# A decoder block on one core: the planner that orders VectorE and ScalarE gets other transfer times and deadlines that are spread out

## The chip, the core and the metric

The kernel runs on one core of a Trainium2 chip. A core has five engines, each with an instruction stream of its own that runs strictly in order: TensorE (PE in the profile; its weight loads are listed as PEld), VectorE (DVE), ScalarE (ACT), GpSimd (POOL) and SyncE (SP). SP and POOL issue nearly all of this kernel's DMAs; the issues themselves are rows SPq, POOL and ACTq. The engines wait for each other, and for DMAs, with semaphores: an instruction whose input is not there holds back everything behind it on its own engine.

The metric is the device time of one execution in microseconds, the median of several runs. The output must agree with the reference.

## The reference, cut to what matters

One decoder block (DEPTH is 1) on 512 tokens with a width of 2048, all in float32:

```python
D_MODEL = 2048; SEQ = 512; MLA_HEADS = 8; GDN_HEADS = 8; D_FF = 5632

c_act = silu(c)
mod = c_act @ w_ada + b_ada                      # six vectors of 2048
sh_a, sc_a, gt_a, sh_f, sc_f, gt_f = split(mod, 6)
h = rmsnorm(x, norm_mix) * (1 + sc_a) + sh_a
p = h @ w_in                                     # queries, keys, values, gates of both mixers
y_a = mla(...) @ w_o_mla                         # latent attention, causal softmax
y_b = gated_delta_net(...) @ w_o_gdn             # chunked gated delta rule
g_a, g_b = split(sigmoid(gate_logits), 2)
x = x + gt_a * ((g_a * y_a + g_b * y_b) @ w_o)
h = rmsnorm(x, norm_ffn) * (1 + sc_f) + sh_f
gate, up = split(h @ w_gate_up, 2)               # w_gate_up: 2048 x 11264
x = x + gt_f * ((silu(gate) * up) @ w_down)      # w_down: 5632 x 2048
return rmsnorm(x, final_norm)
```

## The kernel before

**Precision and tiling.** Activations lie transposed in SBUF, 128 features on the partitions and the 512 tokens along the row. Every float32 operand of a large product is cut in two rounded halves: ScalarE casts a tile to float32r (`hi`, `xh`), VectorE subtracts that from the tile and keeps the rest (`lo`, `xl`). TensorE then does three products for each pair, hi with hi, hi with lo, lo with hi (`three`, line 566). So before a weight tile can be used it goes through a chain: a load on SP's queue into a buffer `raw` or `raws` (five of them, `RAWS`), a cast on ScalarE into one of four `hi` buffers, and a subtraction on VectorE into one of four `lo` buffers (`SPLITS`).

**Strassen products.** The products with w_o, w_gate_up and most of w_down are done in Strassen form, seven products in place of eight (`strassen`, line 2284, for w_o and w_down; `big`, line 2087, for w_gate_up). In `strassen` a unit of work, of which there are eight for each set of 512 output columns, loads one weight tile `raws` of 128x1024 (four blocks of 256 columns). VectorE adds up combinations of the blocks into a tile `sums`; then both are cut in halves: a `hi` and a `lo` of 128x768 from `raws`, a `hi` and a `lo` of 128x1024 from `sums`. The matmuls of this stage write the banks `m`: rows `m<-xh,hi`, `m<-xh,lo` and `m<-xl,hi`. The activation side of w_down's product is made by `sums_down`: it loads blocks `a11`, `a21`, `a22`, `a12` from a scratch tensor in DRAM, `f_dram` (`fetch_a`; rows `a<-f_dram`), adds them up into combinations, and cuts each of these in `xh` (ScalarE) and `xl` (VectorE). The same four tile names hold both the loaded block and a combination of it. The part of w_down that isn't in Strassen form (banks `dn`) ends with four ScalarE instructions `y<-dn,gt_ffn`, which empty its four banks, and four accumulating DMAs into `x2_dram`.

**Stages in time.** First the modulation and the statistics of x (`head`; a product with w_ada is a custom VectorE instruction, `rawm<-rawm,cbc`, of which there are 192; they are spread over the kernel as side work wherever VectorE has room), then w_in with both mixers, among it attention, 32 items of one head and 128 queries each (`attention`, line 1450). An item's probabilities are transposed on TensorE (bank `pT`), copied to SBUF by VectorE or ScalarE in turn (`pT<-pT`), and multiplied with the values (`yT<-pT,V`). Then w_o in Strassen form, whose last set adds into the tiles `x2` (`x<-g`, `x<-p`; the plain remainder of it is `x<-wo`) and squares them (`squares`, tile `sq`) for the norm; a matmul with ones (`hss`) adds up the squares, and VectorE makes the reciprocal root (`rs`). Then w_gate_up, w_down, and the last norm with the output in rows.

**What sets the order.** No engine call is issued where the code makes it. `Writer` (line 287) records each as an `Op` in `Score`; `Op.durations` (line 165) gives it two numbers, `pace`, how long it keeps its engine, and `seen`, when its result can be used. At the end `Score.issue` (line 449) does three things:

- `depend` (line 294) finds from the accesses which operation needs which. Two accesses of one DRAM tensor meet when their ranges overlap.
- `latest` (line 333) gives each operation a deadline. TensorE's operations are due when TensorE would get to them if it ran without a pause; everything else is due early enough for its users, with a DMA's lead put at 2200 ns + bytes/300.
- `order` (line 362) runs through a model of the engines. TensorE, GpSimd and SyncE keep the order in which the code recorded them. For VectorE and ScalarE (`CHOSEN`, line 276) it takes, of the operations that are ready within `LOOK` of the engine's next free moment, the one with the earliest deadline. In this model one bus carries all DMAs at 355 bytes per ns, and a DMA's issue costs 60 ns on SyncE and 600 ns on GpSimd.

The result is a fixed order for each engine, in which the operations are issued (line 454). So nearly all instructions have line 454 in the profile, and groups are told apart by tile. Since the real order is fixed, what the model got wrong turns up on the chip as an instruction that waits at the head of its engine while others behind it could run.

## Time and profile before

| what | us |
|---|---|
| median of the runs | 2729.58 (three runs, 2728.38 to 2730.99) |
| the profiled execution's own time | 2729.74 |
| its span, first to last instruction | 2728.0 |
| TensorE busy | 2703.5, 99% of the span |
| TensorE weight loads busy | 2352.9, 86% |
| VectorE busy | 2128.4, 78% |
| ScalarE busy | 1209.8, 44% |
| GpSimd busy | 254.5, 9% |
| mean granted TensorE clock | 0.997 |

The profiled execution took 1.74 us more than its span, which is what lies before the first and behind the last instruction. The page shows an engine's busy time over the span; the chain of work that ended last is followed back from the last instruction. The view of waits sums, for an engine, the time in which it stood still and what released it. The timeline lists instructions with their start and length in us and, in brackets, the idle time in front of them and its releaser; neighbours of one kind are drawn together as "x3". A table of windows gives busy time, the number of instructions and the granted clock of stretches of time. Names in the trace have no buffer numbers; a tile made in place of a pool named `raws` or `a11` is written `raws` or `a`.

### The profile page before, as it was taken

The page shows a single profiled execution, that of the slowest core. Times are in us where ns is not written, and L with a number is a line of the kernel's source. Part 1 is how long each engine was busy: PE and PEld are TensorE (multiplying, and loading weights), DVE is VectorE, ACT ScalarE, POOL GpSimd, SP SyncE. Part 2 cuts the span into 40 slices and gives each one's busy share as a digit, 9 for nine tenths or more (in the row PEclk, how much of TensorE's full clock was granted, in tenths as well). Part 3 has the DMA queues.
Part 4 walks back from the last instruction along what each step waited for, and adds up shares of the span by engine and source line. Part 5 has one row for each costly group of instructions (what it writes and reads, how often), then busy time and mean ns, then how long its engine had stood idle before and what let it go on. Part 6 is the DMA issues. An engine that isn't in the chain of part 4 may idle for free.

```text
span 2728.0 us, 41132 instructions
## 1 busy us (share of the span) xinstructions
PE 2703.5 (99%) x15304; PEld 2352.9 (86%) x15304; DVE 2128.4 (78%) x3361; ACT 1209.8 (44%) x1717; POOL 254.5 (9%) x361
## 2 busy tenths in 40 slices
PE   9999999999999999999999999999999999999997
PEld 7888788888888888889999888888888888998997
DVE  8885666776978887688797877788878886877976
ACT  4343432442345343245573444444444455445444
POOL 0000011102101000000000000000000103013013
PEclk9999999999999999999999999999999999999999
DMA  9995555645667998524855556666565668569565
GB/s 354 349 371 181 164 179 153 213 141 165 193 177 218 319 320 298 185 88 122 279 178 160 185 198 201 207 206 207 198 212 187 217 212 186 130 195 200 144 186 166
DMA packets 315490, 562.21 MB, mean 206 GB/s; under 512 B 40772, under 2 KB 120916, under 8 KB 315288
## 3 DMA queue, kind: packets, MB, share of 16 engines
q1 hardware_dynamic: 264776, 458.99, 51.7%
q0 software_dynamic: 31872, 74.76, 10.7%
q10 hardware_dynamic: 18640, 25.83, 2.7%
q8 instruction: 120, 1.97, 0.3%
q14 instruction: 82, 0.67, 0.1%
HBM read 476.62 MB, written 83.89 MB: 205 GB/s over the span
## 4 chain that ended last, share of the span: by engine, by line
PE 95%; DMA 2%; DVE 1%; issue 1%; ACT 0%; POOL 0%; SPq 0%; POOLq 0%; ACTq 0%; DVEq 0%
PE m L454 42%; PE gb L454 6%; PE v L454 4%; PE gu L454 3%; PE z L454 3%; PE ya L454 3%; PE ga L454 3%; PE k L454 3%; PE s L454 3%; PE q L454 3%; PE yb L454 3%; PE dn L454 3%; PE qk L454 2%; PE cq L454 2%; PE ckv L454 2%; PE wo L454 1%
## 5 line engine op out<-in xcount | busy, mean ns | idle before, releaser
L454 ACT CAST hi<-raw 128x1024 fp32r<-128x1024 f32 (+2 forms) x251 | 260.3, 1038 | 482.2 <-DMA raw<-in_w_in_dram 92.5
L454 ACT CAST hi<-raws 128x1024 fp32r<-128x1024 f32 (+2 forms) x328 | 292.0, 890 | 398.3 <-PE m L454 289.2
L454 DVE TENSOR_TENSOR lo<-raws,hi 128x1024 fp32r<-128x1024 f32 (+2 forms) x328 | 332.1, 1021 | 127.6 <-ACT hi L454 124.2
L454 DVE TENSOR_TENSOR lo<-raw,hi 128x1024 fp32r<-128x1024 f32 (+2 forms) x251 | 304.5, 1215 | 126.0 <-ACT hi L454 121.5
L454 PE MATMUL m<-xh,lo 128*128 128x256 f32 x1088 | 309.7, 285 | 2.4 <-DVE lo L454 2.4
L454 PE MATMUL m<-xh,hi 128*128 128x256 f32 x1088 | 309.3, 284 | 1.9 <-ACT hi L454 1.9
L454 PE MATMUL m<-xl,hi 128*128 128x256 f32 x1088 | 308.9, 284 | 0.0
L454 DVE CUSTOM_DVE_ANT_0 rawm<-rawm,cbc 128x1024 f32<-128x1024 f32 x192 | 233.1, 1225 | 89.3 <-DMA rawm<-in_w_mod_dram 84.2
L454 ACT CAST hi<-sums 128x1024 fp32r<-128x1024 f32 x168 | 176.4, 1050 | 229.2 <-PE m L454 197.7
L454 DVE TENSOR_TENSOR lo<-sums,hi 128x1024 fp32r<-128x1024 f32 x168 | 205.5, 1223 | 74.0 <-ACT hi L454 72.7
L454 PEld LDWEIGHTS m<-xh,lo 128*128 128x128 f32 x1088 | 209.9, 193 | 3.7 <-DVE lo L454 3.5
L454 PEld LDWEIGHTS m<-xh,hi 128*128 128x128 f32 x1088 | 209.9, 193 | 2.5 <-ACT hi L454 2.4
L454 PEld LDWEIGHTS m<-xl,hi 128*128 128x128 f32 x1088 | 209.9, 193 | 0.1
L454 PE MATMUL m<-hi,h2h 128*128 128x512 f32 x480 | 189.9, 396 | 0.0
L454 PE MATMUL m<-hi,h2l 128*128 128x512 f32 x480 | 187.2, 390 | 0.0
L454 PE MATMUL m<-lo,h2h 128*128 128x512 f32 x480 | 187.1, 390 | 0.0
L454 PEld LDWEIGHTS m<-hi,h2l 128*128 128x128 f32 x480 | 90.1, 188 | 18.8
L454 PEld LDWEIGHTS m<-lo,h2h 128*128 128x128 f32 x480 | 90.3, 188 | 17.8
L454 PEld LDWEIGHTS m<-hi,h2h 128*128 128x128 f32 x480 | 90.2, 188 | 17.6
L454 PE MATMUL gb<-hh,hi 128*128 128x512 f32 x256 | 102.1, 399 | 0.0
L454 PE MATMUL gb<-hl,hi 128*128 128x512 f32 x256 | 100.0, 391 | 0.0
L454 PE MATMUL gb<-hh,lo 128*128 128x512 f32 x256 | 99.8, 390 | 0.0
(543 smaller groups left out, 7018.1 us busy)
## 6 DMA issues: line engine op xcount, KB each, us to landing
raws<-in_w_gate_up_dram SPq DMA_DIRECT2D x400, 256.0 KB, 3.6
rawm<-in_w_mod_dram SPq DMA_DIRECT2D x192, 512.0 KB, 5.4
raw<-in_w_in_dram SPq DMA_DIRECT2D x143, 512.0 KB, 4.7
raws<-in_w_down_dram SPq DMA_DIRECT2D x128, 256.0 KB, 3.7
s_dram<-raws POOLq DMA_DIRECT2D x80, 256.0 KB, 2.6
raws<-s_dram SPq DMA_DIRECT2D x80, 256.0 KB, 2.8
rawa<-in_w_in_dram SPq DMA_DIRECT2D x32, 512.0 KB, 4.5
raws<-in_w_o_dram SPq DMA_DIRECT2D x48, 256.0 KB, 2.9
```

What stands on the lines that cost most here:

```text
L454: self.tc.keep_in_program_order(op.call(*op.args, **op.kwargs))
```

## The change

All of it is in the recorder and the planner; no engine call of the kernel body is added, removed or given other operands.

- **Times of DMAs in the model.** A DMA's issue costs 540 ns on GpSimd (720 when it accumulates), 370 on ScalarE and 410 on SyncE, in place of 600 and 60. A new method `transfer` gives the time on the bus, `move`: bytes/360, times 1.85, 1.5 or 1.17 where the shortest contiguous row of the access is at most 256, 512 or 1024 bytes, and times 2.35 or 3.1 when the DMA accumulates. In `order` a DMA gets to the bus 1200 ns (GpSimd) or 1800 ns after its start, and counts as done 640 ns + `SPARE` (1000) behind its end on the bus.
- **DRAM accesses.** `Access` notes the shortest contiguous row, and for a DRAM tensor keeps the exact stretches in place of one range from the first to the last element.
- **Deadlines.** A DMA's lead is `LANDING` (3000) + `move`. `latest` runs three rounds (`ROUNDS`). After each, the deadlines on VectorE, and those on ScalarE, are gone through from the last back: none may be later than the deadline behind it less the operation's own pace. The next round takes these as caps, and so passes them on to what feeds the operation.
- **LOOK** goes from 400 to 800 ns.

```diff
     def durations(self):
         if self.dma:
-            return (600.0 if self.engine == "gpsimd" else 60.0), 0.0
+            pool = 720.0 if self.kwargs.get("accum_op") is not None else 540.0
+            return {"gpsimd": pool, "scalar": 370.0}.get(self.engine, 410.0), 0.0
...
+    def transfer(self):
+
+        row = min(a.row for a in self.reads + self.writes)
+        if self.kwargs.get("accum_op") is not None:
+            return self.bytes / 360.0 * (3.1 if row > 2048 else 2.35)
+        return self.bytes / 360.0 * (1.85 if row <= 256 else 1.5 if row <= 512 else 1.17 if row <= 1024 else 1.0)
...
-            self.parts, self.runs = (0, 1), ((off, off + sum((c - 1) * abs(s) for s, c in steps) + 1),)
+            self.parts, self.runs = (0, 1), () if self.input else self.stretches(off, steps)
...
     CHOSEN = ("vector", "scalar")
-    LOOK = 400.0
+    LOOK = 800.0
+    LANDING = 3000.0
+    ROUNDS = 3
+    SPARE = 1000.0
...
-        end, out, after = t + 5000.0, [0.0] * n, {}
-        for k in range(n - 1, -1, -1):
-            op = ops[k]
-            seen = 2200.0 + op.bytes / 300.0 if op.dma else op.seen
-            v = min([out[j] - seen for j in self.users[k] + late[k]], default=end)
-            if op.pe:
-                v = start[k]
-            elif op.engine not in self.CHOSEN:
-                v = after[op.engine] = min(v, after.get(op.engine, end) - op.pace)
-            out[k] = v
+        end, cap = t + 5000.0, [t + 5000.0] * n
+        for _ in range(self.ROUNDS):
+            out, after = [0.0] * n, {}
+            for k in range(n - 1, -1, -1):
+                op = ops[k]
+                seen = self.LANDING + op.move if op.dma else op.seen
+                v = min([out[j] - seen for j in self.users[k] + late[k]], default=end - seen)
+                if op.pe:
+                    v = start[k]
+                elif op.engine not in self.CHOSEN:
+                    v = after[op.engine] = min(v, after.get(op.engine, end) - op.pace)
+                out[k] = min(v, cap[k])
+            for e in self.CHOSEN:
+                at = end
+                for k in sorted((k for k in range(n) if ops[k].engine == e), key=lambda k: (-out[k], -k)):
+                    cap[k] = at = min(out[k], at - ops[k].pace)
         return out
...
             if op.dma:
-                bus = max(start + op.pace + 1500.0, bus) + op.bytes / 355.0
-                done[k] = bus + 500.0
+                bus = max(start + (1200.0 if op.engine == "gpsimd" else 1800.0), bus) + op.move
+                done[k] = bus + 640.0 + self.SPARE
```

**What moves.** Both kernels hold the same instructions. The orders of TensorE, GpSimd and SyncE are the same in both. On VectorE 2010 of 3361 instructions stand at another place, on average by two places and at most by 138; on ScalarE 548 of 1801, at most by 18. Three places, with the buffer numbers left in the names:

Place A is ScalarE where the plain part of w_down (`dn36_3`) ends and the Strassen product with w_down begins. `hi_3660` is the cast of the first unit's weights and `hi_3662` that of their sums; `hi_3673` and `hi_3675` belong to the second unit. The `xh` copies cut activation blocks that come from `f_dram` or are made from such blocks. Before:

```order
L454 COPY xh_3683_3823<-a21_3623_3763 128x512
L454 COPY xh_3693_3833<-a11_3618_3758 128x512
L454 COPY hi_3660_3800<-raws_3609_3749 128x768
L454 COPY xh_3698_3838<-a12_3654_3794 128x512
L454 ACTIVATE y_3655_3795<-dn36_3_3637_3777,gt_ffn_120 128x512
L454 ACTIVATE y_3656_3796<-dn36_3_3638_3778,gt_ffn_120 128x512
L454 ACTIVATE y_3657_3797<-dn36_3_3639_3779,gt_ffn_120 128x512
L454 COPY hi_3662_3802<-sums_3659_3799 128x1024
L454 COPY xh_3710_3850<-a11_3682_3822 128x512
L454 ACTIVATE y_3658_3798<-dn36_3_3640_3780,gt_ffn_120 128x512
L454 COPY hi_3673_3813<-raws_3630_3770 128x768
L454 COPY xh_3718_3858<-a12_3700_3840 128x512
```

After:

```order
L477 COPY hi_3660_3800<-raws_3609_3749 128x768
L477 COPY xh_3693_3833<-a11_3618_3758 128x512
L477 COPY xh_3683_3823<-a21_3623_3763 128x512
L477 ACTIVATE y_3655_3795<-dn36_3_3637_3777,gt_ffn_120 128x512
L477 ACTIVATE y_3656_3796<-dn36_3_3638_3778,gt_ffn_120 128x512
L477 ACTIVATE y_3657_3797<-dn36_3_3639_3779,gt_ffn_120 128x512
L477 COPY hi_3662_3802<-sums_3659_3799 128x1024
L477 COPY xh_3698_3838<-a12_3654_3794 128x512
L477 ACTIVATE y_3658_3798<-dn36_3_3640_3780,gt_ffn_120 128x512
L477 COPY hi_3673_3813<-raws_3630_3770 128x768
L477 COPY xh_3710_3850<-a11_3682_3822 128x512
L477 COPY hi_3675_3815<-sums_3672_3812 128x1024
```

`hi_3660` now stands ahead of `xh_3693` and `xh_3683` (which precede it before), and `y_3658` and `hi_3673` stand ahead of `xh_3710`, which preceded both. The next Strassen set of w_down shows the same exchange: `xh_4092` and `xh_4096`, which stood ahead of `y_4047`, `hi_4062` and `hi_4064`, now follow these, and `xh_4100` now follows `hi_4079`, ahead of which it stood. Call that place B.

Place C is VectorE at the end of w_o, ahead of the reciprocal root `rs_2098`, which needs the sum of squares `hss_2097` and so both last additions into `sq_2034`. `g1` and `p1` are Strassen results, `wo3` the banks of the remainder. Before:

```order
L454 TENSOR_TENSOR p1_2019_2159<-euvw_1971,m5_1972_2112 128x512
L454 TENSOR_TENSOR lo_2085_2225<-raw_2062_2202,hi_2084_2224 128x1024
L454 TENSOR_SCALAR x2_2010_2150<-g1_2017_2157,gt_mix_119,x2_2010_2150 128x256 x2
L454 TENSOR_SCALAR x2_2012_2152<-p1_2019_2159,gt_mneg_122,x2_2012_2152 128x256 x2
L454 TENSOR_TENSOR lo_2092_2232<-raw_2069_2209,hi_2091_2231 128x1024
L454 TENSOR_SCALAR x2_2023_2163<-wo3_2027_2167,gt_mix_119,x2_2023_2163 128x256 x2
L454 TENSOR_SCALAR x2_2025_2165<-wo3_2028_2168,gt_mix_119,x2_2025_2165 128x256 x2
L454 TENSOR_TENSOR sq_2034_2174<-sq_2034_2174,sq_2087_2227 128x512
L454 TENSOR_TENSOR sq_2034_2174<-sq_2034_2174,sq_2088_2228 128x512
L454 TENSOR_TENSOR lo_2095_2235<-raw_2076_2216,hi_2094_2234 128x1024
L454 TENSOR_TENSOR lo_2103_2243<-raw_2081_2221,hi_2102_2242 128x1024
L454 TENSOR_SCALAR rs_2098_2238<-hss_2097_2237 128x2
```

After:

```order
L477 TENSOR_TENSOR g1_2017_2157<-euvw_1971,m4_1971_2111 128x512
L477 TENSOR_TENSOR lo_2092_2232<-raw_2069_2209,hi_2091_2231 128x1024
L477 TENSOR_SCALAR x2_2023_2163<-wo3_2027_2167,gt_mix_119,x2_2023_2163 128x256 x2
L477 TENSOR_SCALAR x2_2025_2165<-wo3_2028_2168,gt_mix_119,x2_2025_2165 128x256 x2
L477 TENSOR_TENSOR sq_2034_2174<-sq_2034_2174,sq_2087_2227 128x512
L477 TENSOR_TENSOR sq_2034_2174<-sq_2034_2174,sq_2088_2228 128x512
L477 TENSOR_TENSOR lo_2095_2235<-raw_2076_2216,hi_2094_2234 128x1024
L477 TENSOR_TENSOR lo_2103_2243<-raw_2081_2221,hi_2102_2242 128x1024
L477 TENSOR_SCALAR rs_2098_2238<-hss_2097_2237 128x2
```

`p1_2019` and the two pairs of `x2_2010` and `x2_2012` are gone from this stretch; in the new order they stand behind the whole chain of `rs` and the two `diag_2101` that follow it.

Place D is VectorE in attention; the lines `ISA rawm` are the custom instruction on w_ada, and `pT_1439` is an item's copy of its transposed probabilities. Before:

```order
L454 TENSOR_REDUCE sm_114<-sc_1435_1574 128x1
L454 TENSOR_SCALAR sm_114<-sm_114 128x1
L454 TENSOR_TENSOR lo_1445_1584<-raw_1431_1570,hi_1444_1583 128x1024
L454 ISA rawm_1428_1567,parts_82<-rawm_1428_1567,cbc_128 128x1024
L454 ISA parts_82 128x1
L454 COPY pT_1439_1578<-pT_1438_1577 128x128
L454 TENSOR_TENSOR yl_1437_1576<-yT_1417_1556,yh_1436_1575 128x512
L454 TENSOR_TENSOR sc_1441_1580<-sc_1441_1580,kc_79 128x128
```

After:

```order
L477 TENSOR_SCALAR sm_114<-sm_114 128x1
L477 ISA rawm_1416_1555,parts_82<-rawm_1416_1555,cbc_128 128x1024
L477 ISA parts_82 128x1
L477 ISA rawm_1427_1566,parts_82<-rawm_1427_1566,cbc_128 128x1024
L477 ISA parts_82 128x1
L477 ISA rawm_1428_1567,parts_82<-rawm_1428_1567,cbc_128 128x1024
L477 ISA parts_82 128x1
L477 TENSOR_TENSOR yl_1437_1576<-yT_1417_1556,yh_1436_1575 128x512
L477 COPY pT_1439_1578<-pT_1438_1577 128x128
L477 TENSOR_TENSOR sc_1441_1580<-sc_1441_1580,kc_79 128x128
```

Three custom instructions on w_ada and the `yl` subtraction now stand between the item's `sm_114` and its `pT_1439`; before it was one `lo` and one custom instruction.

At the start of the kernel VectorE now takes a small cast, `strict_r`, ahead of its first custom instruction, and `hl_22`, the second half of the first activation tile, ahead of the wide part of `lo_20`, where it stood behind. At the very end, four of the row products `xo<-x2t,row` now stand between the last two steps of the final norm's `rs`, the three products with `hbc` that followed that chain stand ahead of it, and the last product with `hbc`, `x2_4344`, which stood ahead of two products and one scaling of `xo`, now stands ahead of its last two scalings.

More of the change, by code (lines that the diff above doesn't have):

```diff
@@ L163, in __init__ @@
         self.bytes = 4 * self.writes[0].total
+        self.move = self.transfer() if self.dma else 0.0
     def durations(self):
@@ L213, in __init__ @@
         self.total = self.count * steps[0][1]
+        self.row = 4
+        for s, c in reversed(steps):
+            if c > 1 and 4 * s != self.row:
+                break
+            self.row *= c
         space = str(getattr(t, "space", "")).upper()
```

## The prediction

> **What bounds the kernel now.** I read the page first, then TensorE's waits, then windows around them, then the timeline of each engine there.
>
> ```profile
> PE 2703.5 (99%) x15304; PEld 2352.9 (86%) x15304; DVE 2128.4 (78%) x3361; ACT 1209.8 (44%) x1717; POOL 254.5 (9%) x361
> PE 95%; DMA 2%; DVE 1%; issue 1%; ACT 0%; POOL 0%; SPq 0%; POOLq 0%; ACTq 0%; DVEq 0%
> ...
> PE cb L454 <- DMA crow<-in_c_dram: 3.0, 1, 3.0
> PE m L454 <- DVE lo L454: 2.4, 5, 0.8
> PE m L454 <- ACT hi L454: 1.9, 2, 1.4
> PE hss L454 <- DVE sq L454: 1.2, 2, 0.8
> ```
>
> TensorE is the chain that sets the end, with 95% of it. Its matmuls, their number and their order stay as they are. So the change can win only what TensorE loses in waits and what comes of them, plus something in the tail, and it loses wherever the new order makes TensorE wait. The waits are few. The first 3.0 us (the load of c) is no matter of order. The next three rows, 2.4 + 1.9 + 1.2, are 5.5 us, nearly all of it in three places. But a wait's idle time is not all that it costs:
>
> ```profile
> 2298.00:2309.00 11.00, 8.15 (x41) 0.69 0.46 82
> 2309.00:2320.00 11.00, 11.00 (x95) 1.00 0.42 133
> ...
> 2509.00:2524.00 15.00, 13.62 (x109) 1.00 0.54 124
> 2530.00:2545.00 15.00, 15.00 (x128) 1.00 0.41 118
> ```
>
> These are windows of TensorE's instructions into the banks `m`: length, busy time with the count, granted clock, DMA share, GB/s. In place A (ScalarE's exchange at the start of the Strassen product with w_down) 41 matmuls run in 11 us, where 95 do in the next window. The missing 54 at 11.00/95 = 0.116 us are 6.3 us. In place B, 128 - 109 = 19 are missing, at 15.00/128 = 0.117 us 2.2 us. B kept its clock; A did not.
>
> **The change, part by part.** *Place A.* TensorE, ScalarE, VectorE and SyncE, from the timeline:
>
> ```profile
> 2299.72 0.39 PE L454 MATMUL m<-xh,hi 128*128 128x256 f32 x1 [1.40 <-ACT hi L454]
> 2300.72 0.39 PE L454 MATMUL m<-xh,lo 128*128 128x256 f32 x1 [0.49 <-DVE lo L454]
> ...
> 2302.55 0.41 PE L454 MATMUL m<-xh,lo 128*128 128x256 f32 x1
> ...
> 2304.10 0.58 PE L454 MATMUL m<-xh,hi 128*128 128x256 f32 x1 [0.50 <-ACT hi L454]
> ...
> 2305.36 0.58 PE L454 MATMUL m<-xh,lo 128*128 128x256 f32 x1 [0.46 <-DVE lo L454]
> ...
> 2285.11 0.63 ACT L454 CAST xh<-a 128x512 fp32r<-128x512 f32 x1 [2.24 <-DVE a L454]
> 2285.64 0.83 ACT L454 CAST hi<-raws 128x768 fp32r<-128x768 f32 x1
> ...
> 2297.74 0.62 ACT L454 CAST xh<-a 128x512 fp32r<-128x512 f32 x1 [7.95 <-DMA a<-f_dram]
> 2298.27 0.68 ACT L454 ACTIVATE y<-dn,gt_ffn 128x512 f32<-128x512 f32 x1
> 2298.85 0.82 ACT L454 CAST hi<-raws 128x768 fp32r<-128x768 f32 x1
> ...
> L454 PE MATMUL dn<-ah,lo x18: 389/389/397, 2275.8 to 2287.9; 128*128 128x512 f32 x18
> ...
> 2291.08 0.69 DVE L454 TENSOR_TENSOR sums<-raws 128x512 f32<-128x512 f32 x1
> ...
> 2289.84 2.98 SPq L454 DMA_DIRECT2D a<-f_dram  x4
> ```
>
> ScalarE stood 7.95 us in front of `xh_3710`, whose block was still coming. Behind it stood `y_3658` and `hi_3673`, which could have run: the last matmul into the `dn` banks started at 2287.9, and VectorE read that unit's `raws` at 2291.08. So the cast for the second unit ended at 2299.67, TensorE ran dry at 1.40 us, and the `lo` behind it cost another 0.49. Then the third unit's tiles were late as well (0.50, 0.46), and in between the clock halved: a matmul takes 0.41 in place of 0.28.
>
> Now `y_3658` and `hi_3673` stand ahead of `xh_3710`. With the input there from 2291.8 at the latest, both can run some 6 us before TensorE wants them at 2298.1, so the first two waits have nothing left in them. `hi_3660` also moves up past two `xh` (0.53 each, the distance of 2297.74 and 2298.27). Its row at 2285.64 stands behind an `xh` that itself waited 2.24, so it runs between 1.1 and 3.3 us earlier. Its `raws` buffer comes free as much earlier, and with that the load of the next unit and, behind this in SyncE's queue, the four `a` loads of 2289.84. That is the cover for the third unit. If it were gone, 0.50 and 0.46 would stay. I take the 6.3 us and leave one wait of the smallest size seen, 0.46: gain 5.8. The bounds are 6.3 and, if the clock falls all the same, 2.3 (the first two gaps; rival 1).
>
> *Place B.* The same exchange:
>
> ```profile
> 2524.06 0.39 PE L454 MATMUL m<-xh,lo 128*128 128x256 f32 x1 [0.75 <-DVE lo L454]
> ...
> 2507.06 0.62 ACT L454 CAST xh<-a 128x512 fp32r<-128x512 f32 x1 [6.60 <-DMA a<-f_dram]
> 2507.59 0.68 ACT L454 ACTIVATE y<-dn,gt_ffn 128x512 f32<-128x512 f32 x1
> 2508.17 0.82 ACT L454 CAST hi<-raws 128x768 fp32r<-128x768 f32 x1
> ```
>
> Here `xh_4092` held up the same pair for 6.60 us, and later `xh_4100` stood ahead of `hi_4079`, whose `lo` released the 0.75. Both now stand behind. Of the 2.2 us I leave 0.3: gain 1.9, bounds 0.75 and 2.2.
>
> *Place C*, the norm behind w_o, on VectorE, with TensorE last:
>
> ```profile
> 1342.86 0.68 DVE L454 TENSOR_TENSOR p<-euvw,m 128x512 f32<-128x512 f32 x1
> ...
> 1344.59 0.87 DVE L454 SCALAR_TENSOR_TENSOR x<-g,gt_mix,x 128x256 f32<-128x256 f32 x2
> 1345.38 0.87 DVE L454 SCALAR_TENSOR_TENSOR x<-p,gt_mneg,x 128x256 f32<-128x256 f32 x2
> ...
> 1347.32 1.65 DVE L454 SCALAR_TENSOR_TENSOR x<-wo,gt_mix,x 128x256 f32<-128x256 f32 x4
> ...
> 1350.42 1.05 PE L454 MATMUL hss<-ones,sq 128*128 128x1 f32 x8 [0.77 <-DVE sq L454]
> ```
>
> The first three of these leave the stretch ahead of the squares: 0.60 + 0.79 + 0.80 (each to the start of the next instruction) make 2.2 us. The wait was 0.77, so it goes whole: gain 0.8, bounds 0 and 0.8. The three are taken behind the norm's root; `p1` reads the bank `m5`, which so comes free later, and a later set may need it, which is why the lower bound is 0.
>
> *Start.* `hl` moves ahead of the wide `lo`:
>
> ```profile
> 10.42 0.96 DVE L454 TENSOR_TENSOR lo<-raw,hi 128x768 fp32r<-128x768 f32 x1 [0.55 <-ACT hi L454]
> ...
> 12.10 0.50 PE L454 MATMUL s<-hl,hi 128*128 128x512 f32 x1 [0.53 <-DVE hl L454]
> ```
>
> `hl` waits for ScalarE's `hh`, which gave TensorE its own matmul only 1.04 us before; it can so win a part of the 0.53, and the wide `lo`, now behind it, is wanted a matmul later. I take 0.2, between 0 and 0.5. `strict_r` goes into time in which VectorE waits for the first load: nothing.
>
> *Place D*, attention, as one instance of a cost: side work on w_ada moves ahead of an item's copy.
>
> ```profile
> 950.58 1.22 DVE L454 CUSTOM_DVE_ANT_0 rawm<-rawm,cbc 128x1024 f32<-128x1024 f32 x1
> ...
> 951.72 0.29 DVE L454 COPY pT<-pT 128x128 f32<-128x128 f32 x1
> 951.92 0.68 DVE L454 TENSOR_TENSOR yl<-yT,yh 128x512 fp32r<-128x512 f32 x1
> ...
> 954.81 0.38 PE L454 MATMUL yT<-pT,V 128*128 128x128 f32 x2
> ...
> L454 DVE COPY pT<-pT x16: 281/421/558, 862.7 to 997.6; 128x128 f32<-128x128 f32 x8, 128x384 f32<-128x384 f32 x8
> ```
>
> Ahead of `pT_1439` there were a `lo` and one custom instruction, about 2 x 1.14 us apart; now there are three and `yl`, 3 x 1.14 + 0.60. That is 1.7 us more, and the copy's user starts 2.8 us after the copy's end at 952.01. So here it is hidden, with 1.1 us over. A single further custom instruction (1.14) would just use that up, and the 16 such copies and their kin do not all have this slack. I set against the change 0.6, half of one such instruction, between 0 and 1.2.
>
> *Tail.* The last `x` product now comes later in VectorE's order by three instructions, but GpSimd stood idle before the last issue:
>
> ```profile
> 2723.03 0.73 POOL L454 DMA_DIRECT2D out_dram<-x  x1 [1.49 <-issue]
> ```
>
> The four `xo` products moved behind the reduction fill no gap any more, the three `x` products moved up do. I book 0, between a gain of 1.5 (this idle time) and a loss of 0.7 (one product of 0.68).
>
> *The rest* of the 2010 and 548 moved instructions lie where TensorE waits for nothing (no row in its list of waits) and move two places on average; they are booked at 0, covered by buffers already filled. If that cover fails somewhere, the 0.6 of D has to stand for it.
>
> Sum: 5.8 + 1.9 + 0.8 + 0.2 - 0.6 + 0 = 8.1 us. From the profiled execution's 2729.74 that is 2721.6; the median of the runs shown, 2729.58, lies 0.16 lower, which I leave out.
>
> [...] In place A the granted clock was 0.69 over 11 us, after idle stretches of 1.40 and 0.49 us. [...]
>
> **The rivals.** *1. A wait stays in A and the clock still falls.* The `a` loads are late again, since the longer queue of loads is the same, and the second pair of waits (0.50, 0.46) and the half clock stay. Only the two first gaps go: 1.40 + 0.49 and 0.2 of slower restarts beside them and their neighbours, about 2.3. Sum 8.1 - 5.8 + 2.3 = 4.6, so 2725.1. For it: the block of `xh_3710` came 7.95 us late, far more than what `hi_3660` gains. Against it: PE's third unit needed its weights, not that block.
>
> *2. The half clock has another cause than the waits.* The waits in A go, 1.40 + 0.49 + 0.50 + 0.46 and about 0.7 around them, 3.5; the slow matmuls stay. Sum 8.1 - 5.8 + 3.5 = 5.8: 2723.9. B's waits with the clock at 1.00 speak for neither side. [...]
>
> *3. The waits only move.* The planner still knows nothing of what the chip does; the casts wait for other blocks, as `xh` does in A now, and gains of A and B (7.7) come back as losses elsewhere. 2729 to 2730. Against it: in the new order no `xh` of those waiting stands ahead of a due `hi` in A and B.
>
> *4. Slower: attention.* VectorE is busy 78% of the span, and side work now comes in groups ahead of softmax steps. An item on VectorE that gets its copy 0.26 us too late at each of the 32 items would eat the 8.1 (8.1/32 = 0.25); from there on the kernel is slower. With a delay of 1.7 us as at D, and a slack of 1.1 in place of 2.8 at the others, it is 0.6 x 32 = 19 us, 2721.6 + 19 = 2741. Against it: the one slack looked at is 2.8, and no attention row is in TensorE's waits.
>
> **How the numbers follow.** Chances: forecast 0.68, rival 1 0.12, rival 2 0.05, rival 3 0.08, rival 4 0.07. The forecast's own bounds: all gains at their best (6.3 + 2.2 + 0.8 + 0.5 + 1.5) make 2718.4, with D at 1.2 and small gains in B and C 2724. The range 2719 to 2727 leaves out rival 4, rival 3 and the best corner. About 0.2% of the time, 5.5 us, is what a measurement here can tell from no change: faster is below 2724.1, slower above 2735.0. Faster: 0.68 and rival 2, 0.05, 0.73. Same: rivals 1 and 3, 0.20. Slower: 0.07.
>
> **What would show it.** Right: TensorE's list of waits loses its rows for `hi` and the 0.8 of `hss`; the window after the w_down start has about 95 matmuls in 11 us and the clock at 1.00; ScalarE's wait of 7.95 us for `a` shrinks and stands behind `y` and `hi`. Wrong: a new row of waits for `lo` or `pT`, a clock below 1.00 in any window, or waits for banks behind the norm. The forecast is wrong as a whole if TensorE's waits in attention come to more than 3 us.

## The result, and the profile after

The changed kernel takes 2718.44 us (median of six runs, 2718.29 to 2720.25), against 2730.24 for the kernel before in the six runs beside it: a ratio of 0.9958 with a 95% interval of 0.9946 to 0.9971. The profiled execution's span fell from 2728.0 to 2716.5 us, by 11.4 us. The forecast was 8.1 us less, 2721.6, with a range from 2719.0; the time lies 0.6 us below that range.

TensorE's list of waits after:

```profile
PE cb L477 <- DMA crow<-in_c_dram: 3.1, 1, 3.1
PE s L477 <- ACT hh L477: 1.1, 1, 1.1
PE hss L477 <- DVE sq L477: 0.3, 1, 0.3
PE s L477 <- DVE hl L477: 0.3, 1, 0.3
```

All waits of the banks `m` are gone, and the longer one for `hss`. TensorE now runs from its first product to its last nearly without a pause; the chain that ended last is 99% TensorE, against 95%. The windows of TensorE's instructions into `m`, at the places A (first two rows) and B, with the columns as in the prediction:

```profile
2290.00:2301.00 11.00, 11.00 (x94) 1.00 0.89 193
2301.00:2312.00 11.00, 11.00 (x94) 1.00 0.43 120
2497.00:2512.00 15.00, 15.00 (x128) 1.00 0.54 126
2512.00:2527.00 15.00, 15.00 (x128) 1.00 0.35 106
```

ScalarE at A after the change:

```profile
2281.22 0.84 ACT L477 CAST hi<-raws 128x768 fp32r<-128x768 f32 x1 [0.20 <-PE dn L477]
...
2288.21 0.69 ACT L477 ACTIVATE y<-dn,gt_ffn 128x512 f32<-128x512 f32 x1
2288.92 0.83 ACT L477 CAST hi<-raws 128x768 fp32r<-128x768 f32 x1
2291.04 0.62 ACT L477 CAST xh<-a 128x512 fp32r<-128x512 f32 x1 [1.28 <-DMA a<-f_dram]
2291.80 1.05 ACT L477 CAST hi<-sums 128x1024 fp32r<-128x1024 f32 x1
```

The wait of 7.95 us for a block is 1.28 us, and it stands behind `y` and `hi`.

Both traces hold the same 15304 TensorE instructions in the same order. So one can take the start of each in one trace from its start in the other, and see where before falls behind. In the profiled execution of before these losses are: start 0.25, attention 0.26, C 1.02, A 6.35, B 2.52, a second `hss` near the end 0.19; and from the last matmul to the end 14.48 against 13.57 us, 0.91. Together 11.5, with 0.1 gained back at the start. The experiments are read with the same difference, always against the kernel after. The 0.25 of the start is no more than scatter: at 30 us, TensorE lies between 0.28 us ahead of after and 0.57 us behind it over all the profiles below, whichever order the start has.

### The profile page after: what moved, and what is told of

Same layout as the page of the kernel before. It is cut to its first block, busy times and chain, and to the rows that moved or that the text cites. A ratio compares the mean times of both kernels' runs of the same rounds, so it can differ in the third digit from the quotient of the medians.

```text
span 2716.5 us, 41153 instructions
## 1 busy us (share of the span) xinstructions
PE 2698.4 (99%) x15304; PEld 2349.9 (87%) x15304; DVE 2130.9 (78%) x3361; ACT 1213.8 (45%) x1717; POOL 257.7 (9%) x361
## 4 chain that ended last, share of the span: by engine, by line
PE 99%; issue 0%; DVE 0%; DMA 0%; SPq 0%; ACT 0%; POOLq 0%; DVEq 0%
PE m L477 44%; PE gb L477 6%; PE v L477 4%; PE gu L477 3%; PE z L477 3%; PE ya L477 3%; PE ga L477 3%; PE k L477 3%; PE s L477 3%; PE dn L477 3%; PE q L477 3%; PE yb L477 3%; PE wo L477 2%; PE qk L477 2%; PE cq L477 2%; PE ckv L477 2%
## 5 line engine op out<-in xcount | busy, mean ns | idle before, releaser
L477 ACT CAST hi<-raw 128x1024 fp32r<-128x1024 f32 (+1 forms) x251 | 260.4, 1038 | 473.0 <-DMA raw<-in_w_in_dram 81.5
L477 DVE TENSOR_TENSOR lo<-raw,hi 128x1024 fp32r<-128x1024 f32 (+1 forms) x251 | 303.7, 1211 | 166.5 <-ACT hi L477 163.7
```

Source lines behind the costliest of these rows:

```text
L477: self.tc.keep_in_program_order(op.call(*op.args, **op.kwargs))
```

## The experiments

The kernel before doesn't repeat as well as the kernel after: its 115 runs beside the experiments lie between 2724.68 and 2740.22, median 2729.64. A single exchange is therefore read place by place from its profile, and the times say less.

| kernel | median us (runs) | ratio to before, 95% | attention | C | A | B | tail |
|---|---|---|---|---|---|---|---|
| before, its profile | 2730.24 (6) | | 0.26 | 1.02 | 6.35 | 2.52 | 0.91 |
| a_pair | 2730.41 (8) | 0.9991 to 1.0014 | 0.76 | 4.96 | 6.45 | 3.34 | 0.92 |
| a_hi | 2730.49 (8) | 0.9994 to 1.0017 | 1.10 | 0.91 | 3.46 | 3.77 | 0.91 |
| a_pair_sums | 2727.31 (8) | 0.9982 to 1.0005 | 0.09 | 0.78 | 0 | 3.10 | 0.94 |
| a_full | 2727.52 (8) | 0.9979 to 1.0002 | 1.69 | 1.93 | 0 | 4.42 | 0.91 |
| b_full | 2727.35 (8) | 0.9977 to 0.9999 | 1.85 | 3.54 | 1.79 | 0 | 0.92 |
| c_act | 2727.45 (8) | 0.9978 to 0.9999 | 1.11 | 0 | 1.99 | 3.25 | 0.92 |
| c_p1 | 2728.13 (8) | 0.9984 to 1.0004 | 1.10 | 0 | 1.93 | 2.77 | 0.93 |
| first_half | 2730.57 (8) | 0.9982 to 1.0009 | 0 | 3.63 | 3.34 | 3.00 | 0.92 |
| tail_only | 2727.27 (8) | 0.9980 to 1.0006 | 2.17 | 1.15 | 1.22 | 3.81 | 0.01 |
| act3 | 2722.00 (8) | 0.9956 to 0.9979 | 1.35 | 0 | 0 | 1.17 | 0.91 |
| spread_only | 2728.70 (10) | 0.9991 to 1.0010 | 1.87 | 2.73 | 4.23 | 2.97 | 0.92 |
| times_only | 2718.51 (5) | 0.9949 to 0.9978 | 0 | 0 | 0 | 0 | 0 |
| look400 | 2718.54 (4) | 0.9947 to 0.9977 | 0 | 0 | 0 | 0 | 0 |
| no_spread | 2718.53 (4) | 0.9947 to 0.9977 | 0 | 0 | 0 | 0 | 0 |
| bus | 2720.76 (6) | 0.9951 to 0.9976 | 0.33 | 0 | 0 | 0 | 1.09 |
| nobus | 2724.18 (10) | 0.9971 to 0.9990 | 0 | 0.33 | 0 | 2.28 | 0 |
| bus_spare | 2723.57 (10) | 0.9970 to 0.9989 | 2.33 | 0 | 0 | 2.45 | 1.09 |
| bus_accum | 2723.39 (10) | 0.9964 to 0.9984 | 1.24 | 0 | 0 | 0 | 0.92 |

The columns of places are us that TensorE lost there against the profile of after, one profile for each kernel. What it lost elsewhere isn't in the table: 2.7 us around the second `hss` in a_hi, 3.0 in nobus, 4.8 with a late `x2` in bus_accum, 1.4 or less in the others; up to 0.9 (first_half) at the start of `dn`; and 1.6 of a slower clock at 804 us in c_p1, first_half and bus (last section). The median stands beside that of before in the same set of runs, which lies between 2728.2 and 2730.6; the ratio takes that into account.

**How single pieces were exchanged.** The kernel plans both orders, and gives VectorE or ScalarE, between two positions of its sequence, the operations in the order of after; the sets between the positions are the same in both. All else has the order of before.

```diff
+    def issue(self):
+
+        old, new = self.planned(True), self.planned(False)
+        for e in self.CHOSEN:
+            for lo, hi in PICK[e]:
+                assert set(old[e][lo:hi]) == set(new[e][lo:hi]), (e, lo, hi)
+                old[e][lo:hi] = new[e][lo:hi]
+        for k in self.order(old):
```

### Place A in pieces

```diff
 a_pair       PICK = {"vector": (), "scalar": ((1458, 1461),)}
 a_hi         PICK = {"vector": (), "scalar": ((1450, 1453),)}
 a_pair_sums  PICK = {"vector": (), "scalar": ((1458, 1464),)}
 a_full       PICK = {"vector": ((2588, 2705),), "scalar": ((1413, 1475),)}
```

> The order of before, with one piece of place A exchanged: y_3658 and hi_3673 ahead of xh_3710. The forecast's theory (these two behind a late block are what makes TensorE run dry, and the first two gaps go): about 2.4 us less from 2298 on, gaps of 0.50 and 0.46 left, 2727.5 in all. Rival (hi_3675, which still stands behind xh_3718 and xh_3714 and their blocks, sets the next cast at 2303.0 whatever the pair does): the gaps of 1.40 and 0.49 go, but TensorE waits as much longer at the next cast, and the gain by 2309 is under 1 us, clock apart.

> The order of before, with one piece of place A exchanged: hi_3660 ahead of xh_3693 and xh_3683. The forecast's theory (this move is only the cover for the third unit): the gaps of 0.50 and 0.46 go, the 1.40 stays, and the gain is about 1 us without the clock, about 3 us with it. Rival (the move lets SyncE issue the four loads of f_dram some 3 us earlier, and with them comes everything behind them on ScalarE): the 1.40 and 0.49 go too, the wait of 7.95 us on ScalarE becomes about 5, and the gain is 4 to 6 us.

> As the pair alone, and hi_3675 ahead of xh_3718 and xh_3714 as well; hi_3660 and the loads stay late. If the casts behind late blocks are the whole cause, TensorE's waits in place A go without any earlier load: gain 5 to 6.3 us. If the late loads themselves count, waits for the third unit of about 1 us remain and the clock falls: gain 2 to 4 us.

> The order of before, with that of after in place A alone, on ScalarE and VectorE. If the gain of place A is its own, TensorE's lead over before is 6.3 us behind it and the clock stays at 1.00 there; the waits of place B and C stay. If the new order before it prepared it, less than 5.

ScalarE in before, behind the cast `hi_3673` that the prediction shows; the second row is `hi_3675`, behind the copies `xh_3718` and `xh_3714`:

```profile
2301.97 1.14 ACT L454 CAST xh<-a 128x512 fp32r<-128x512 f32 x2 [2.29 <-DMA a<-f_dram]
2303.01 1.04 ACT L454 CAST hi<-sums 128x1024 fp32r<-128x1024 f32 x1
```

It ended at 2304.05, and the matmul that waited 0.50 us for a `hi` started at 2304.10. So the waits of 0.50 and 0.46, which the prediction gave to the third unit, are the second unit's sums. ScalarE in a_pair:

```profile
2294.70 0.85 ACT L519 CAST hi<-raws 128x768 fp32r<-128x768 f32 x1
2300.75 0.62 ACT L519 CAST xh<-a 128x512 fp32r<-128x512 f32 x1 [5.20 <-DMA a<-f_dram]
2305.07 1.14 ACT L519 CAST xh<-a 128x512 fp32r<-128x512 f32 x2 [3.71 <-DMA a<-f_dram]
2306.11 1.04 ACT L519 CAST hi<-sums 128x1024 fp32r<-128x1024 f32 x1
```

and TensorE there, then its windows:

```profile
2307.21 0.39 PE L519 MATMUL m<-xh,hi 128*128 128x256 f32 x1 [2.46 <-ACT hi L519]
2308.46 0.58 PE L519 MATMUL m<-xh,lo 128*128 128x256 f32 x1 [0.76 <-DVE lo L519]
```

```profile
2298.00:2309.00 11.00, 7.79 (x61) 0.95 0.76 176
2309.00:2320.00 11.00, 11.00 (x73) 0.74 0.31 97
```

`hi_3673` was cast in time, and it gained nothing: TensorE gets through the matmuls that use it and stands before those of the next cast, `hi_3675`, which two copies with late blocks still hold up; it waits 2.46 us there in place of 1.40 and 0.49 earlier. A costs 6.45 us. The forecast's reading of the pair is refuted. The profiles with the old order at A say the same: in b_full, c_act, c_p1 and tail_only TensorE has no wait for `hi_3673` or its `lo`, and only the later ones, for `hi_3675` and its `lo`, are left (0.71 and 0.76 in c_act). a_pair_sums also takes `hi_3675` past `xh_3718` and `xh_3714`, and A costs nothing, though ScalarE still stands 4.66 us before the block of `xh_3710`. a_full does no more than that. So the exchange that counts takes `hi_3675` along, and an earlier load, which the forecast called the cover, isn't needed for it. `hi_3675` without the pair was not run.

a_hi was to try the earlier load alone, but the load doesn't come earlier:

```profile
2290.13 2.92 SPq L519 DMA_DIRECT2D a<-f_dram  x4
```

TensorE is 0.64 us later there than in before, where the four loads go out at 2289.84, so they are 0.35 us earlier against TensorE, not the 1.1 to 3.3 of the forecast; in c_act, with the old order there, they are 1.6 us earlier, so this is scatter. SyncE's load ahead of them starts at 2288.10, when VectorE's `lo` of a `raws` tile ends (2288.07), and VectorE has the order of before. So moving `hi_3660` alone brings no cover. Nor do the 3.46 us that a_hi loses at A show a gain: the six other profiles with the old order there lose 1.22 to 4.23.

Earlier loads are another way, though. In nobus (below) `hi_3660` stands behind three `xh` copies in place of four, the four loads go out 3.8 us earlier against TensorE than in before, and `xh_3710` still stands ahead of `hi_3673`, `xh_3718` and `xh_3714` ahead of `hi_3675`:

```profile
2285.49 2.52 SPq L477 DMA_DIRECT2D a<-f_dram  x4
```

```profile
2291.99 0.62 ACT L477 CAST xh<-a 128x512 fp32r<-128x512 f32 x1 [2.72 <-DMA a<-f_dram]
2292.51 0.83 ACT L477 CAST hi<-raws 128x768 fp32r<-128x768 f32 x1
```

A costs nothing there either: the block comes after 2.72 us, and TensorE needs the cast only some 4 us after its end.

### Place B alone, and three pieces of ScalarE alone

```diff
 b_full  PICK = {"vector": ((2838, 2918),), "scalar": ((1583, 1621),)}
 act3    PICK = {"vector": (), "scalar": ((861, 873), (1458, 1464), (1610, 1615), (1619, 1621))}
```

> The order of before with that of after in place B alone, on ScalarE and VectorE. TensorE loses nothing at 2509 to 2530, 2.2 to 2.6 us less than before there; the waits of A and C stay.

> The order of before with three pieces of ScalarE's order alone from after: hi_2053 ahead of a21h_2063 (20 us ahead of C); y_3658, hi_3673 and hi_3675 ahead of the late xh (A); the same at B. VectorE's order is that of before. If a cast held up behind a late block is the cause in all three places: no wait for hi or lo in A and B, no wait over 0.4 us for the hss of C, and 8 to 9.9 us less than before; attention and tail stay as before, so 2719.5 to 2722. Rival (VectorE's new order is needed too): 2723 or more, waits for lo left in B.

b_full loses nothing in B, and keeps its losses in A and C. act3 has VectorE's old order throughout; its waits on TensorE:

```profile
PE m L519 <- DVE lo L519: 0.8, 1, 0.8
PE gb L519 <- DVE yl L519: 0.6, 1, 0.6
...
PE hss L519 <- DVE sq L519: 0.3, 1, 0.3
```

A and C are gone, and B falls to 1.17: one wait for `lo` is left, where VectorE's order stayed, as the rival had it for B. The median is 2722.0, at the upper edge of the first expectation. Pieces of ScalarE's order at three places, 25 positions in all, carry 7.6 of the 11 us.

### Place C: what made VectorE late

VectorE stood in before, 13 us ahead of the stretch that the prediction shows; then ScalarE, which it waited for:

```profile
1329.66 1.23 DVE L454 TENSOR_TENSOR lo<-raw,hi 128x1024 fp32r<-128x1024 f32 x1 [3.75 <-ACT hi L454]
```

```profile
1327.38 1.30 ACT L454 CAST a21h<-a 128x512 fp32r<-128x512 f32 x2 [3.59 <-DMA a<-a_dram]
...
1328.59 1.05 ACT L454 CAST hi<-raw 128x1024 fp32r<-128x1024 f32 x1
```

That is the same picture as in A: two copies `a21h` of a block that is still coming, ahead of a cast. The runs part this from the move of `p1`:

```diff
 c_act  PICK = {"vector": (), "scalar": ((861, 873),)}
 c_p1   PICK = {"vector": ((1700, 1768),), "scalar": ((877, 919),)}
```

> The order of before, with one piece on ScalarE exchanged, some 20 us ahead of the place where hss waits: hi_2053 ahead of a21h_2063 and a21h_2065, which wait for a load. The forecast's theory (what counts in C is p1 and the x2 pairs on VectorE): the wait of 0.8 us or more for sq stays. Rival (VectorE is late at C because ScalarE stood 3.6 us before a21h): TensorE's wait for sq falls to 0.3 us or less, and its step there is 0.9 us or more less than before.

> The order of before, with p1_2019 and the x2 pairs behind rs_2098 on VectorE and what goes with them; a21h_2063 stays ahead of hi_2053. The forecast's theory: 2.2 us of work leave the stretch and the wait for sq goes, 0.9 us. Rival: VectorE's lateness stays, but it is 2.2 us shorter, so the wait goes too where it was under 2 us; then both ways are sufficient, and neither alone is the cause.

Either way C is at 0, against 0.78 to 4.96 in the profiles with the old order there, so each is enough alone; in c_p1 ScalarE still stands 3.57 us before `a21h`. ScalarE in c_act:

```profile
1325.51 1.05 ACT L519 CAST hi<-raw 128x1024 fp32r<-128x1024 f32 x1 [0.78 <-PE wo L519]
1328.19 0.62 ACT L519 CAST a21h<-a 128x512 fp32r<-128x512 f32 x1 [1.10 <-DMA a<-a_dram]
```

times_only and look400 keep `p1` and the `x2` pairs ahead of the root, as before, and lose nothing in C. What the forecast named works, but it isn't needed.

### Start, attention and the tail

```diff
 first_half  PICK = {"vector": ((0, 1655),), "scalar": ((0, 861),)}
 tail_only   PICK = {"vector": ((3055, 3168),), "scalar": ((1706, 1779),)}
```

> The order of after up to the end of w_o's first sets, so start and attention, with the order of before behind. Forecast's D: attention costs 0.6 us. Against it, from the trace of after: yl comes sooner, the waits of gb and yT for yl and pT (0.2 to 1.7 us from run to run before) go, and TensorE's lead over before at 1000 us is 0.3 to 1.5 us; A, B and C keep their waits.

> The order of before with the last part, from the row products on, from after. The forecast's 0 for the tail: the stretch from the last matmul to the end stays as before within 0.3 us. Against it, from the trace of after: it is 0.9 us shorter. A, B and C keep their waits.

Attention in the order of before cost 0.09 to 2.17 us in the ten profiles that have it; a_full's shows one such wait, on TensorE, then on VectorE:

```profile
973.00 0.47 PE L519 MATMUL gb<-hh,hi 128*128 128x512 f32 x1 [0.46 <-DVE yl L519]
```

```profile
970.83 0.29 DVE L519 COPY pT<-pT 128x128 f32<-128x128 f32 x1
971.03 1.22 DVE L519 CUSTOM_DVE_ANT_0 rawm<-rawm,cbc 128x1024 f32<-128x1024 f32 x1
...
972.17 0.69 DVE L519 TENSOR_TENSOR yl<-yT,yh 128x512 fp32r<-128x512 f32 x1
```

and VectorE at the same item in after:

```profile
968.46 0.29 DVE L477 COPY pT<-pT 128x128 f32<-128x128 f32 x1 [0.33 <-PE pT L477]
...
969.82 0.69 DVE L477 TENSOR_TENSOR yl<-yT,yh 128x512 fp32r<-128x512 f32 x1 [0.81 <-ACT yh L477]
```

The custom instruction between `pT` and `yl` is gone. first_half loses nothing in attention. The three custom instructions of place D did no harm: in after the copy's user starts at 954.65 and the copy ended at 952.50. The tail is 13.58 us in tail_only, as in after, and 14.48 to 14.50 in every kernel with VectorE's old end (14.66 in bus and bus_spare, which have an end of their own). The traces of before and after show where the 0.91 lies. GpSimd's last issue, of `out_dram<-x`, doesn't move: it starts 9.54 us behind the start of the last matmul in before and 9.58 in after. But its transfer lands sooner. Its time from issue to landing, in before and then in after:

```profile
DMA to landing us min/median/max: 3.5/3.5/3.5
DMA to landing us min/median/max: 2.6/2.6/2.6
```

In before three more stores of `x` leave GpSimd in the 3.7 us ahead of that issue; in after the store before it left 7.2 us earlier. That these three are why the last one takes longer fits, but was not tried alone.

### Parts of the planner

```diff
 spread_only (before, deadlines spread)
-        for k in range(n - 1, -1, -1):
+        for _ in range(3):
...
 times_only (after, LOOK = 400.0 too)
-    ROUNDS = 3
+    ROUNDS = 1
...
 look400 (after)
-    LOOK = 800.0
+    LOOK = 400.0
...
 no_spread (after)
-    ROUNDS = 3
+    ROUNDS = 1
```

> The planner of before with the three rounds that spread out the deadlines, and nothing else. Its order keeps xh_3710 ahead of y_3658 and hi_3673, xh_4092 ahead of y_4047 and hi_4062, and p1_2019 ahead of rs_2098. If the transfer times and LOOK are the cause: no change within 2 us, the waits of A, B and C stay. Rival (spreading is what makes the new order): 5 us or more faster, by waits that are not in A to C.

> The new times and accesses of DMAs without spreading (one round) and with LOOK at 400. Its order has the exchanges of A and B, with hi_3675 and hi_4079 ahead of the late xh, but p1_2019 and x2 stay ahead of rs_2098. If place by place holds: 6.3 and 2.5 us from A and B, the wait for hss in C stays: about 2720.5. Rival (the parts only work together): under 5 us of gain.

> The kernel after with LOOK at 400 in place of 800. A and B as after, p1_2019 and x2 ahead of rs_2098 as before. About 1 us slower than after (the wait for hss comes back), in all about 2719.5. Rival: LOOK also matters at many small places, 3 us or more slower than after.

> The kernel after with one round, so without spreading. A, B and C as after. If spreading is worth nothing: within 0.5 us of after, 2718.5. Rival (it keeps side work in attention or the tail off the path): 1 to 3 us slower, with waits for pT, yl or in the tail.

Spreading alone is worth nothing (2728.70 beside 2728.20), and taking it out costs nothing. The same holds for LOOK: look400 was expected 1 us slower than after and isn't, since C doesn't hang on `p1`. All is in the times of DMAs. They were parted further; nobus has all of the new times but those of `order`, the other three start from the planner of before (cut to the lines that count):

```diff
 bus (nobus is times_only without this)
-                bus = max(start + op.pace + 1500.0, bus) + op.bytes / 355.0
-                done[k] = bus + 500.0
+                bus = max(start + (1200.0 if op.engine == "gpsimd" else 1800.0), bus) + op.move
+                done[k] = bus + 640.0 + self.SPARE
...
 bus_spare
-                done[k] = bus + 500.0
+                done[k] = bus + 1640.0
...
 bus_accum
-                bus = max(start + op.pace + 1500.0, bus) + op.bytes / 355.0
+                bus = max(start + op.pace + 1500.0, bus) + op.bytes / 355.0 * (2.75 if op.kwargs.get("accum_op") is not None else 1.0)
```

> The planner of before with the new end times of DMAs in order alone (start, move, 640 + SPARE); issue costs, DRAM stretches, deadlines and LOOK of before. If the blocks that come late are planned too early for want of a right end time, this alone has the whole effect: 2718.5 to 2720, no waits in A, B and C. Rival (issue cost or lead times are needed as well): 2723 or more.

> All the new times but those of order: issue costs, DRAM stretches, leads. xh_3710 stays ahead of hi_3673 and xh_4092 ahead of hi_4062. If the end times are the cause: the waits of A and B stay, 2726 to 2730. Rival: 2723 or less.

> The planner of before with one number changed: a DMA counts as done 1640 ns behind its end on the bus in place of 500 (the 640 and the 1000 of SPARE). If a plain allowance for lateness is enough, the waits of C and A go (hi_2053 and hi_3673 stand ahead of the late blocks; at B xh_4092 still stands ahead of hi_4062), and the whole is 2719 to 2722. Rival (the factors of transfer, the accumulations above all, are what counts): 2724 or more.

> The planner of before with one number changed: an accumulating DMA keeps the bus 2.75 times as long. If the accumulations in front of the loads from f_dram are why these come late, C goes and A goes in part (hi_3675 stands ahead of xh_3718, xh_3710 still ahead of hi_3673): 2720 to 2724. Rival: as before within 2 us, since the two late blocks keep their place.

The end times in `order` alone clear A, B and C. The median of 2720.76 lies just above the expectation; in the profile 0.33 of attention, 1.09 of the tail and 1.57 us of a slower clock (last section) are left. nobus missed its expectation, in time (2724.18 is between the two) and in A, as told above; it keeps B, and loses 3.0 at the second `hss`. But its attention and its tail are those of after: these two gains come with the other new times (issue costs, DRAM stretches, leads), not with the end times. Each half of the new end times does a good part: bus_spare clears C and A, where `hi_3673` now precedes the late block, and not B, where `xh_4092` still precedes `hi_4062`; a copy with a late block still stands ahead of `hi_3675`. bus_accum clears all three, more than expected, though `xh_3710` keeps its place; `hi_3675` has moved. It loses 4.8 us at the end, at the second `hss` and a late `x2`. In both, and in bus, the four loads of A also go out 3.9 to 4.0 us earlier against TensorE than in before, so A is cleared there by both ways together or by the loads alone. Neither half is the whole: 2723.57, above the expected 2719 to 2722, and 2723.39. The trace of before fits both. The loads of `f_dram` and the accumulating DMAs into `x2_dram`, of 256 KB each, take at the median, from issue to landing,

```profile
a<-f_dram SPq DMA_DIRECT2D x32, 256.0 KB, 6.7
x_dram<-y POOLq DMA_DIRECT2D x32, 256.0 KB, 7.4
```

and the old model, with an empty bus, says 60 + 1500 + 262144/355 + 500 = 2798 ns for the first and 3338 ns for the second.

## Why the prediction was right or wrong

- **What bounds it** was right: TensorE's waits and the tail are all that the change could win, no new wait came, and A, B and C are where most of it was. The steps that put the time outside the range are those on attention and the tail, and what was left over in A, B and C.
- **Place A** was booked at 5.8 of 6.3; 6.35 were lost there in the profiled execution, and all came back. The 0.46 left for a wait that stays was caution, and no wait stayed. The mechanism was half right. `y_3658` and `hi_3673` ahead of `xh_3710` alone give nothing (a_pair); the step that failed is "so the first two waits have nothing left in them", which looked at one cast and not at the next, `hi_3675`, behind the same late loads: what leaves the first two waits comes back there, as 2.46 us. The waits of that next cast were read as the third unit's, and `hi_3660` was named as their cover; moved alone, it brings the loads 0.35 us (a_hi). The order showed the exchange that was needed too, in the row after `xh_3710`.
- **Place B** was booked at 1.9; it gave 2.52. The upper bound, 2.2, was too low: the matmuls were counted in a window that is shorter than the stretch, and the last slow steps in before lie at 2529.3 and 2529.5, 5 us behind its end. The reading of ScalarE's rows holds (b_full, act3).
- **Place C** was booked at 0.8 and gave 1.02; the idle time of 0.77 leaves out the rest of the step: from the start of the last `wo` ahead of `hss` to the first `hss` it is 1.04 us in before and 0.12 in after, and the eight `hss` take 0.92 us to the next matmul in place of 0.82. The cause named, `p1` and `x2` in VectorE's way, is enough (c_p1) but not what made VectorE late; that was a wait of 3.59 us on ScalarE some 20 us earlier. The step that failed read the stretch just ahead of the wait and didn't ask why VectorE had no slack there.
- **Attention**: -0.6 was wrong in sign. It gains 0.26 in the profiled execution. The step took one place where side work moves forward, found it hidden, and charged for others unseen. The place where side work stood in front of `yl` was in the order and in the trace and wasn't looked for, since TensorE came only 0.16 us late there in that profile, which made no row in its list of waits.
- **Tail**: 0 was wrong, it gains 0.91. The bounds given (1.5 to -0.7) hold it, but not for their reason: the idle time of 1.49 us ahead of GpSimd's last issue was to shrink, and that issue starts as late as before (9.58 us behind the last matmul's start, against 9.54); its transfer lands sooner, 2.6 us after the issue in place of 3.5.
- **The sum**: 5.8 + 1.9 + 0.8 + 0.2 - 0.6 + 0 = 8.1; in measured terms 6.35 + 2.52 + 1.02 + 0.25 + 0.26 + 0.91 + 0.19 = 11.5. Of the 3.4 missing, 1.8 are the tail and attention's sign, 1.4 what was left over in A, B and C, mostly out of caution, and the last 0.2 are the second `hss` and the start. The range's low end of 2719.0 left out just the corner where all goes well at once. The terms aren't independent, so that corner is less rare than it looks: the new end times alone clear A, B and C (bus), and the other new times alone bring attention and the tail (nobus).
- **The rivals.** 1 and 3 didn't occur. (The 2.3 of rival 1 is not the sum of its terms, 1.40 + 0.49 + 0.2 = 2.1; with 0.2 at each of the two gaps it is.) Against rival 2, a half clock that is not due to the waits, speaks that in the windows at A of after, a_full, a_pair_sums and act3, which have no waits there, the granted clock is 1.00, and that the seven other kernels without waits there lose nothing at A. With waits it was 0.69 in before and 0.74 in a_pair, in the 11 us behind its wait of 2.46, but 1.00 in a_hi. Rival 4, attention slower, is refuted: after has no row of waits there, and first_half loses nothing against it.
- One thing that fits by chance: the profiled execution of before lost more in A than the six other profiles with the old order there (1.22 to 4.23), and less in B, C and attention than most. That it stands for the medians' difference of 11 us all the same is because these deviations cancel. So the 5.8 of A is the size of one execution. By the medians, whose intervals are some 3 us wide to either side, A alone is worth 2.0 and 2.2 us (a_full, a_pair_sums), B 2.3 (b_full), C 3.1 and 2.5 (c_act, c_p1), and the tail 2.4 (tail_only), where its profile shows 0.9.

## What to carry to other kernels

Here a planner fixes the order ahead of time, and its errors in transfer times turned up as an instruction at the head of ScalarE's queue that waits for a late block, 7.95 us at A, 6.60 at B and 3.59 ahead of C, with due work behind it. In such a kernel, look for the long waits on the engine that feeds the busiest one, even where that engine is 44% busy, and follow a small wait of TensorE back over several instructions before naming its cause. When one piece of an order is judged, go on to the next thing that the consumer needs: here clearing one cast of a chain moved the wait (2.46 us in a_pair); clearing the next one too removed it (A costs 0 in a_pair_sums), and so did loads that came 3.8 us earlier (nobus).

## What the hardware showed that was not expected

**The clock.** In before the granted clock was 0.50 for 6.8 us, from 2301.8 on, behind idle stretches of TensorE of 1.40 and 0.49 us; those of 0.50 and 0.46 fall in that time. In a_pair it fell at about 2307.8, behind the 2.46: it was 0.95 from 2298 to 2309 and 0.74 from 2309 to 2320. In a_hi TensorE idled for 0.49, 1.30 and 0.75 us and kept its clock, 1.00:

```profile
2303.30 0.39 PE L519 MATMUL m<-xh,hi 128*128 128x256 f32 x1 [1.30 <-ACT hi L519]
2304.56 0.39 PE L519 MATMUL m<-xh,lo 128*128 128x256 f32 x1 [0.75 <-DVE lo L519]
```

```profile
2298.00:2309.00 11.00, 8.46 (x66) 1.00 0.53 103
```

The closest pair is at C: TensorE waits 1.66 us for `hss` in a_pair and in a_full, and from 1352 to 1359 us its granted clock, with TensorE's busy time and instructions before it, is, in a_pair and then in a_full:

```profile
1352.00:1359.00 7.00, 7.00 (x35) 0.51 0.75 245
1352.00:1359.00 7.00, 6.48 (x54) 1.00 0.86 282
```

So behind the same wait of 1.66 us the clock was 0.51 in one profile and 1.00 in the other; what decides between the two was not shown. A half clock is part of what C and A cost in the table: a_pair lost 4.96 us at C, and a_full, with the same wait, 1.93; and the 6.35 of before at A include what the 6.8 us at 0.50 cost.

The clock also fell at one place without any wait. In three of the twenty profiles (c_p1, which has the order of before at that place, first_half, which has that of after, and bus, which has its own) it was at 0.57 to 0.62 from 804 to 808 us with TensorE busy throughout, at 1.6 us of cost. In bus, then in before:

```profile
804.00:808.00 4.00, 4.00 (x12) 0.57 0.35 95
```

```profile
804.00:808.00 4.00, 4.00 (x23) 1.00 0.36 95
```

What sets it off wasn't tried.

**Scatter.** before's 115 runs span 15.5 us; the 19 of after, times_only, look400 and no_spread, whose TensorE waits for nothing but the start and 0.3 us of `hss`, span 2.1 (2718.20 to 2720.25). The numbers of runs differ, but so do the standard deviations, 2.3 against 0.6 us. Here the kernel with the waits for late transfers has the wider spread, besides the longer time.
